# One engine order for the whole kernel: a list scheduler in the kernel in place of the built-in order (hybrid encoder layer, one core)

## The chip, the core and the metric

The kernel runs on one core of a Trainium2 chip. Five engines work side by side, each through its own queue in order: TensorE (PE in the profile; PEld is its weight loads), VectorE (DVE), ScalarE (ACT), GpSimd (POOL) and SyncE (SP, which here only issues DMAs). The metric is the device time of one execution in microseconds, lower is better.

## What is computed

One layer of a streaming encoder, for a prompt of 512 rows and a sample of 64 rows (together T = 576 columns) with shared weights, in fp32:

```python
D_MODEL = 1024; SEQ = 512; DEC_SEQ = 64; CHUNK = 64; N_MEM = 256; D_FF = 4096
xn = _rmsnorm(x, ln_mix);  proj = xn @ w_in
conv_in, z, a, b, qd, kd, vd = jnp.split(proj, SPLIT_AT, axis=-1)
c = jax.nn.silu(_causal_conv(conv_in, conv_w, conv_buf))            # 12 blocks of 128 channels
g = -jnp.exp(a_log) * jax.nn.softplus(a + dt_bias);  beta = jax.nn.sigmoid(b)
oa, S_new = _gdn_chunked(qa, ka, va, g, beta, S0)                    # gated delta rule, 4 heads, chunk by chunk
ob = _diff_attention(qd, k_all, v_all, q_pos, k_pos, lam)            # softmax minus lam * softmax, 4 heads
h = x + concat[rmsnorm(oa) * silu(z), rmsnorm(ob) * (1 - lam0)] @ w_out
h = h + _mem_attn(_rmsnorm(h, ln_mem_q), mem_k, mem_v, w_mem_q, w_mem_o)   # mem_k, mem_v from rmsnorm(mem_prompt)
h = h + jnp.square(jax.nn.relu(_rmsnorm(h, ln_ffn) @ w_ff1)) @ w_ff2
y = _rmsnorm(h, ln_final)
```

## The kernel before

Activations are held transposed (channels on partitions, 576 columns). Each fp32 operand of a large product is split into a high part and a rest, both in the fast fp32 form (`wh` and `wl` for weights, made from `raw` by a ScalarE cast on L159 and a VectorE subtraction on L160; `u_6`, `u_7` for the activations). `project` (L167) makes one block of 128 output channels in a PSUM bank with tag `pr`, in two halves of the columns: the first 256 with high and rest side by side (512 wide for `wh`, 256 for `wl`), and the other 320 one after the other. All matmuls are issued by `mm` (L107), all transposes by `tr` (L113), so the trace shows these two lines for nearly everything on TensorE, and the tile names tell the work: `pr` is a projection, `g0`, `g1` are the banks of the delta-rule preparation and later of the attention scores, `gs` the bank of the delta-rule scan and of the attention output, `ba` the transposes.

The stages in the profiled execution: to about 36 us the head block (norm of x, first projections), to 97 the convolution inputs, to 131 the gates and z, to 247 the delta rule (`gdn_prep` L653, `gdn_scan` L814) with projections beside it, to 357 the differential attention with the remaining input projections and the memory keys and values beside it, to 525 the output projection and the memory attention, to 945 the output of the memory attention and the feed-forward part, then the tail.

What sets the order of the work: the kernel issues instructions in program order, stage by stage, and a built-in scheduler reorders them on every engine by dependences, free buffers and priorities. The kernel steers it at a few places. `in_order` (L52, used once around the head block at L363) chains the instructions of a block on each engine as they are written; `tc.issue_after` (L430, L469, L477, L601, L609, L705, L848, L934, L956, L1458, L1660) keeps a block behind a given instruction; `tc.keep_in_program_order` (L109, L115, L133) pins some matmuls, transposes and two loads; `tc.high_priority` (L158 and others) favours casts. Buffers: three banks for `pr`, two for `ba`, one each for `g0`, `g1`, `gs`; three `raw`, two `wh` and two `wl`.

Lines that the prediction speaks of: L155 loads a weight block into `raw`; L261 to L267 load the small constants; L490 loads the gate columns of `w_in` (`wab`), L514 and L515 `dt_bias` and `a_log` into `dtb`, and L517 is the Exp of `a_log`; L133 loads a gain row for all partitions (`gB`, 512 KB); L286 casts the transposed activations of the head block into `u_6` and `u_7`; L645 belongs to the gates and z.

Of the kernel before, what the change touches and what calls it, by code (L numbers as in the profile page):

```python
# [15 lines left out]
P = 128  # L16
# [19 lines left out]

@with_exitstack
def hybrid_layer_kernel(
# [11 lines left out]

    @contextmanager
    def in_order():  # L52

        block = nc.cur_bb.bb.instructions
        first, last, ends = len(block), {}, {}
        yield ends
        for i in block[first:]:
            if i.engine in last:
                tc.add_manual_dep(
                    i, last[i.engine],  # L60
                    mybir.DependencyInfo(mybir.DependencyClass.NoSync, mybir.DependencyReason.DATA),
                    reason="in_order",
                )
# [3 lines left out]
    cp = ctx.enter_context(tc.tile_pool(name="cp", bufs=1))
    up = ctx.enter_context(tc.tile_pool(name="up", bufs=1))
    tp = ctx.enter_context(tc.tile_pool(name="tp", bufs=2))
    wp = ctx.enter_context(tc.tile_pool(name="wp", bufs=2))  # L70
# [35 lines left out]
    def mm(out, lhsT, rhs, start=True, stop=True, pin=False, skip_group_check=False):  # L106
        i = nc.tensor.matmul(out, lhsT, rhs, start=start, stop=stop, skip_group_check=skip_group_check)  # L107
        if pin:
            tc.keep_in_program_order(i)  # L109

    def tr(out, in_, pin=False):
        n = in_.shape[0]
        i = nc.tensor.transpose(out, in_, ident[:n, :n])  # L113
        if pin:
            tc.keep_in_program_order(i)  # L115
# [92 lines left out]
    def row_broadcast(rst, out, pin=False):  # L208

        b, b2 = bank(), bank()  # L210
        for t in range(5):
            o = b2[:, :P] if t == 4 else b[:, t * P : (t + 1) * P]
            mm(o, bc(rst[:, t : t + 1], [P, P]), ident, pin=pin and t % 4 == 0)
        A.copy(out[:, :SEQ], b)
        V.tensor_copy(out[:, SEQ:], b2[:, DEC:P])
        return out
# [146 lines left out]
    with in_order() as opened:  # L363
# [78 lines left out]
    for typ in (1, 0, 2):  # L442
        flat = (e5[:, 1], e2[:, 1], e2[:, 0])[typ].rearrange("p k t -> p (k t)")

        cT[typ] = [ap.rearrange("p (h t) -> p h t", h=H) for ap in (flat[:, : H * SEQ], flat[:, H * SEQ :])]
        for h in range(H):
            m = typ * 4 + h
            if m in FIRST:
                if m != FIRST[0]:
                    second(m)  # L450
            else:
                project(weights(w2, m * P), xs, conv_input(m))
            cb = cbs[m]
# [6 lines left out]
            last_v = nc.cur_bb.bb.instructions[-1]  # L460
# [16 lines left out]
    with tc.issue_after(behind_keys[1]):  # L477
# [117 lines left out]
    tc.keep_in_program_order(nc.sync.dma_start(mt, mem_prompt[0].rearrange("(b p) d -> p b d", p=P)))  # L595
# [5 lines left out]
    with tc.issue_after(behind_keys[1]):  # L601
# [7 lines left out]
    with tc.issue_after(last_v):  # L609
# [43 lines left out]
    def gdn_prep(c, nb, L):  # L653
# [34 lines left out]
        summed[c] = nc.cur_bb.bb.instructions[-1]  # L688
# [16 lines left out]
        with tc.issue_after(summed[0]):  # L705
            for i in range(nb):
                V.scalar_tensor_tensor(gam[:, i, :], bg[:, i, :], G_[:, i : i + 1], most, ALU.subtract, ALU.min)
# [106 lines left out]
    def gdn_scan(c, L, q, S):  # L814
# [32 lines left out]
        def finish():  # L847
            with tc.issue_after(summed[min(c + 2, 4)]):  # L848
                next(norm, None)
# [84 lines left out]
    with tc.issue_after(behind_keys[0]):  # L934
# [21 lines left out]
    with tc.issue_after(behind_keys[0]), tc.issue_after(behind_keys[1]):  # L956
# [389 lines left out]
    fp = ctx.enter_context(tc.tile_pool(name="fp", bufs=1, reuse_waits="tile"))  # L1346
# [124 lines left out]
    def ff1_pair(p, sx):  # L1471
# [58 lines left out]
        put_last[p] = nc.cur_bb.bb.instructions[-1]  # L1530
# [77 lines left out]
    def final_roots(ts, pin=False, more=None):  # L1608
# [3 lines left out]
        for i, t in enumerate(ts):  # L1612
            q0, n = QT[t]
            mm(b[:, t : t + 1], accs[0][:, q0 : q0 + n], ones[:, 0:1], pin=pin and i == 0)
# [38 lines left out]
    for g in range(1, NG):  # L1653
        nxt = odd() if g % 2 else pair(5, F32R)
        for m in range(KT):
# [3 lines left out]
            if g == 2:  # L1659
                with tc.issue_after(nc.cur_bb.bb.instructions[-1]):  # L1660
# [61 lines left out]
```

## Time and profile before

| | us |
|---|---|
| median of 3 runs | 970.83 (970.36 to 972.32) |
| the profiled execution | 972.5 |
| its span, first to last instruction | 968.8 |
| mean granted TensorE clock | 0.997 |

The times are those of whole executions; the profile is one execution with a span a little shorter than its time. Busy times of the engines overlap, so they don't add up to the span. A matmul's busy time is modelled from its start to the end of its pipeline, so two matmuls in a row overlap. What the rows show is given with the prediction. A row of the timeline is start, length, engine, line, operation, output<-inputs, shape and count; in brackets stand the idle time ahead of it and what ended it.

### The profile page before, as it was taken

Reading aid. Unit: us, or ns where it says so; the run is one execution under the profiler, and the core shown is the slowest. Engines: PE = TensorE matmul, PEld = TensorE weight load, DVE = VectorE, ACT = ScalarE, POOL = GpSimd, SP = SyncE. Lnnn points to the kernel's source line nnn. Section 1 sums busy time; section 2 is a strip of 40 time slices with the busy share of each in tenths; the row PEclk is TensorE's granted clock in tenths of the full one; section 3 lists DMA queues with packets and bytes.
Section 4 is the critical chain, followed back from the end, with each engine's and each line's share of the span. In section 5 each row is a group of like instructions: output and inputs, shape, how many; then the busy total and the mean of one; then the engine's idle time right before and its main releaser. Section 6 shows DMA issues by size and latency. Waiting matters only on the chain.

```text
span 968.8 us, 17030 instructions
## 1 busy us (share of the span) xinstructions
PE 954.5 (99%) x6399; PEld 888.5 (92%) x6399; DVE 689.6 (71%) x1538; ACT 541.3 (56%) x1248; POOL 66.9 (7%) x158
## 2 busy tenths in 40 slices
PE   9999999999999999999999999999999999999996
PEld 7999998998889878999999999999999999999996
DVE  6655777776867776666557977668867779978574
ACT  7664775533656765444445658666645554555444
POOL 4341020211010000000000000000000000000000
PEclk9999999999999999999999999999999999999998
DMA  7442342120643657332112423322322222323202
GB/s 210 123 134 77 87 134 66 38 72 22 177 133 105 224 175 220 87 112 64 44 44 65 123 66 116 90 88 87 88 88 87 88 88 87 88 88 87 66 23 97
DMA packets 124915, 96.01 MB, mean 99 GB/s; under 512 B 6204, under 2 KB 112846, under 8 KB 124322
## 3 DMA queue, kind: packets, MB, share of 16 engines
q1 hardware_dynamic: 124466, 94.28, 33.6%
q8 instruction: 50, 0.82, 0.4%
q10 hardware_dynamic: 368, 0.66, 0.2%
q14 instruction: 31, 0.25, 0.1%
HBM read 79.93 MB, written 9.75 MB: 93 GB/s over the span
## 4 chain that ended last, share of the span: by engine, by line
PE 61%; issue 2%; ACT 0%; POOLq 0%; POOL 0%; DVE 0%; ACTq 0%
PE pr L107 38%; PE ba L107 11%; PE g L107 7%; PE gs L107 4%; PE ba L113 1%; ACT u L1601 0%; POOLq L1718 0%; POOL tiny L206 0%; DVE u L1219 0%; ACTq L1606 0%; DVE tiny L1615 0%; POOLq L206 0%
## 5 line engine op out<-in xcount | busy, mean ns | idle before, releaser
L107 PE MATMUL pr<-u,wh 128*128 128x320 f32 (+2 forms) x1240 | 325.7, 341 | 0.3
L107 PEld LDWEIGHTS pr<-u,wh 128*128 128x128 f32 x1240 | 211.8, 188 | 15.4 <-ACT u L286 0.4
L107 PE MATMUL pr<-u,wl 128*128 128x256 f32 (+1 forms) x816 | 225.8, 300 | 0.0
L107 PEld LDWEIGHTS pr<-u,wl 128*128 128x128 f32 x816 | 150.3, 189 | 2.4 <-DVE wl L387 0.2
L160 DVE TENSOR_TENSOR wl<-raw,wh 128x1024 fp32r<-128x1024 f32 x65 | 79.5, 1224 | 56.4 <-ACT wh L159 56.2
L159 ACT CAST wh<-raw 128x1024 fp32r<-128x1024 f32 x65 | 68.3, 1051 | 61.2 <-PE pr L107 44.6
L107 PE MATMUL pr<-u,w2h 128*128 128x320 f32 (+1 forms) x384 | 96.7, 339 | 0.0
L107 PE MATMUL pr<-f,w2h 128*128 128x320 f32 (+1 forms) x288 | 72.4, 339 | 0.0
L1459 ACT CAST w2h<-r 128x512 fp32r<-128x512 f32 x56 | 34.8, 621 | 65.4 <-PE pr L107 64.1
L107 PEld LDWEIGHTS pr<-u,w2h 128*128 128x128 f32 x384 | 65.1, 188 | 4.3
L107 PE MATMUL pr<-u,w2l 128*128 128x256 f32 (+1 forms) x256 | 65.2, 295 | 0.0
L206 POOL TENSOR_TENSOR tiny<-tiny,nhalf 128x1 f32<-128x1 f32 (+4 forms) x10 | 8.9, 888 | 645.2 <-DVE tiny L1615 508.0
L107 PE MATMUL ba<-u,wl 128*128 128x288 f32 x360 | 52.7, 295 | 0.0
L107 PEld LDWEIGHTS pr<-f,w2h 128*128 128x128 f32 x288 | 48.8, 188 | 3.4 <-issue 0.2
L1549 DVE TENSOR_TENSOR u<-u,pr 128x256 f32<-128x256 f32 x96 | 43.3, 451 | 8.6 <-PE pr L107 7.9
L107 PEld LDWEIGHTS ba<-u,wl 128*128 128x128 f32 x360 | 49.4, 188 | 0.0
L107 PE MATMUL pr<-f,w2l 128*128 128x256 f32 (+1 forms) x192 | 48.8, 295 | 0.0
L107 PEld LDWEIGHTS pr<-u,w2l 128*128 128x128 f32 x256 | 47.0, 189 | 1.5
L1460 DVE TENSOR_TENSOR w2l<-r,w2h 128x512 fp32r<-128x512 f32 x56 | 38.6, 689 | 9.9 <-ACT w2h L1459 9.7
L107 PE MATMUL pr<-wh,u 128*128 128x512 f32 x128 | 41.6, 400 | 0.1
L107 PEld LDWEIGHTS pr<-f,w2l 128*128 128x128 f32 x192 | 35.2, 189 | 1.1
L1506 ACT ACTIVATE c<-c 128x288 f32<-128x288 f32 x48 | 20.3, 445 | 27.2 <-DVE c L1505 26.1
(552 smaller groups left out, 2027.6 us busy)
## 6 DMA issues: line engine op xcount, KB each, us to landing
raw<-in_w_ff_dram SPq DMA_DIRECT2D x36, 512.0 KB
raw<-in_w_in_dram SPq DMA_DIRECT2D x28, 512.0 KB
r<-in_w_ff_dram SPq DMA_DIRECT2D x56, 256.0 KB
raw<-in_w_mem_k_dram SPq DMA_DIRECT2D x8, 512.0 KB
raw<-in_w_mem_v_dram SPq DMA_DIRECT2D x8, 512.0 KB
raw<-in_w_out_dram SPq DMA_DIRECT2D x8, 512.0 KB
raw<-in_w_mem_q_dram SPq DMA_DIRECT2D x8, 512.0 KB
raw<-in_w_mem_o_dram SPq DMA_DIRECT2D x8, 512.0 KB
```

The source lines that it names most:

```text
L107: i = nc.tensor.matmul(out, lhsT, rhs, start=start, stop=stop, skip_group_check=skip_group_check)
L113: i = nc.tensor.transpose(out, in_, ident[:n, :n])
L159: A.copy(wh, raw)
L160: V.tensor_tensor(wl, raw, wh.bitcast(F32), ALU.subtract)
L206: G.tensor_tensor(out, in_, bc(nhalf[: in_.shape[0], 0:1], list(in_.shape)), ALU.pow)
L1459: A.copy(wh, src)
L1460: V.tensor_tensor(wl, src, wh.bitcast(F32), ALU.subtract)
L1506: A.activation(c, c, AF.Relu)
L1549: V.tensor_tensor(am, am, b, ALU.add)
```

## The change

The hints to the built-in scheduler become data, and a scheduler inside the kernel fixes the order of every engine. `in_order` and the new `after` only note chains of instruction names; the pins are gone; pools are wrapped so that each tile's pool, tag and number of buffers are known. At the end of the program `arrange` builds a `Step` for every traced instruction, with its reads and writes, its dependences and an estimated duration, runs a simulated clock over all engines, always taking the instruction that can start first (among those that can start by then on that engine, the one with the best priority, then the earliest in the program), and pins the resulting order of each engine with dependences that carry no semaphore. The number of matmuls, transposes, DMAs, VectorE and GpSimd instructions stays what it was; ScalarE's table loads go from 15 to 13.

The core of the diff:

```diff
+class Step:
...
+    def cost(self):
...
+        if self.engine == "PE":
...
+            self.fetch = 105.0 if self.turn else max(105.0 * w.size / 128, 55.0)
...
+            by_size = {512: 235.0 if len(x.dims) > 2 else 229.0, 384: 175.0, 320: 146.5, 288: 132.5, 256: 119.0}
...
+        elif self.engine == "ACT":
+            self.time = (155 if bank else 190) + 0.84 * n + 100 * (len(self.ins) > 1) + 60 * (len(self.outs) > 1)
+        elif self.engine == "DVE":
...
+                self.time = 145 + 1.06 * n + 62 * (column and self.op == "TensorScalarPtr")
+        else:
+            power = self.op == "TensorTensor" and any(a.tile.startswith("nhalf") for a in self.ins)
+            by_op = dict(TensorTensor=(185, 2.2), TensorScalarPtr=(185, 2.2), TensorScalarAffineSelect=(150, 1.8))
+            base, rate = (500, 140) if power and n <= 16 else by_op.get(self.op, (100, 0.85))
+            self.time = base + rate * n
...
+class Arrangement:
...
+        for _ in range(len(todo)):
+            start, engine = min((self.start(s), e) for e in engines for s in self.queue[e])
+            s = min((s for s in self.queue[engine] if self.start(s) <= start), key=lambda s: (s.priority, s.n))
+            self.queue[engine].remove(s)
+            self.open_tiles(s)
+            end = self.execute(s)
...
+    def start(self, s):
+        at = s.ready
+        for t in s.tiles:
+            at = max(at, self.opened[t] if t in self.opened else min(self.slots[self.place[t][0]]["free"]) + 33)
...
+        if s.engine == "PE":
+            began, step = self.last
+            return max(began + step, max(began, at) + s.fetch)
+        return max(self.clock[s.engine], at)
+
+    def execute(self, s):
...
+        if s.is_dma:
+            self.clock[s.engine] = at + 400
+            begin = max(at + 1300, self.wire)
+            self.wire = begin + s.bytes / 240.0
+            return max(self.wire + 500, at + 1900)
+        if s.engine == "ACT":
+            table = dict(Silu="Silu", Exp="Exp").get(str(getattr(s.inst, "func", "")).split(".")[-1])
+            if table not in (None, self.table):
+                self.table = table
+                at += 1300
+        self.clock[s.engine] = at + s.time - OVERLAP[s.engine]
+        return at + s.time + 10
...
+def arrange(tc, instructions, homes, chains, closing, opening):
+    for instructions_of_engine in Arrangement(instructions, homes, closing, opening, chains).run().values():
+        for earlier, later in zip(instructions_of_engine, instructions_of_engine[1:]):
+            tc.add_manual_dep(
+                later, earlier.name,
+                mybir.DependencyInfo(mybir.DependencyClass.NoSync, mybir.DependencyReason.DATA),
+                reason="arrange",
+            )
...
+    chains, opened = [], {}
+
     @contextmanager
     def in_order():
...
+        for i in block[first:]:
+            engines.setdefault(i.engine, []).append(i.name)
+        chains.extend(engines.values())
+        opened.update((e, names[-1]) for e, names in engines.items())
...
+    def after(*earlier):
+
         block = nc.cur_bb.bb.instructions
...
+        first = len(block)
+        yield
+        chains.extend((e, i.name) for i in block[first:] for e in earlier)
...
-    def mm(out, lhsT, rhs, start=True, stop=True, pin=False, skip_group_check=False):
-        i = nc.tensor.matmul(out, lhsT, rhs, start=start, stop=stop, skip_group_check=skip_group_check)
-        if pin:
-            tc.keep_in_program_order(i)
...
+    def mm(out, lhsT, rhs, start=True, stop=True, skip_group_check=False):
+        nc.tensor.matmul(out, lhsT, rhs, start=start, stop=stop, skip_group_check=skip_group_check)
...
-        tc.keep_in_program_order(nc.sync.dma_start(gB, g.partition_broadcast(P)))
+        nc.sync.dma_start(gB, g.partition_broadcast(P))
...
-    with tc.issue_after(opened[mybir.EngineType.Pool]):
+    with after(opened[mybir.EngineType.Pool]):
...
+
+    arrange(tc, nc.cur_bb.bb.instructions, homes, chains, closing="sp", opening="fp")
```

Below, lines of the changed kernel differ from those of before: L107 is L407 there, L113 is L411, L159 is L455, L286 is L582, L517 is L813.

**TensorE in the delta rule** (around 231 to 238 us in the profile before). `g1_360` to `g1_363` are steps of the preparation of one chunk, `gs_417` and `gs_419` of the scan, `g0_3..` of the preparation of the next chunk, `pr_5..` projections. Before:

```order
L107 MATMUL pr_539_3120<-u_7_92,wh_534_3092 128x320
L113 MATMUL g1_361_2269<-ident_79,Dt1_343_2185 128x128 x4
L113 MATMUL g0_397_2395<-ident_79,X_393_2389 128x128 x2
L107 MATMUL g1_362_2276<-Dt1_343_2185,At1_335_2160 64x64 x4
L107 MATMUL g1_363_2282<-X_341_2183,Y1_342_2184 64x64 x4
L113 MATMUL g0_399_2402<-ident_79,Y0_394_2390 128x128
L107 MATMUL g0_399_2402<-Dt0_395_2391,B0_398_2400 128x128
L107 MATMUL gs_417_2476<-on_416_2474,X_341_2183 128x128 x3
L107 MATMUL g0_400_2407<-Y0_394_2390,X_393_2389 128x128
L107 MATMUL gs_417_2476<-on_416_2474,X_341_2183 128x128
L107 MATMUL gs_419_2483<-S_267_1889,u_4_78 128x128
```

Now:

```order
L407 MATMUL g0_386_2369<-u_1_75 128x128
L411 MATMUL g1_361_2269<-ident_79,Dt1_343_2185 128x128 x4
L407 MATMUL g0_386_2369<-u_1_75 128x128
L407 MATMUL gs_415_2469<-S_267_1889,u_1_75 128x128 x3
L407 MATMUL g1_362_2276<-Dt1_343_2185,At1_335_2160 64x64 x4
L407 MATMUL g0_388_2375<-u_4_78,u_1_75 128x128 x2
L407 MATMUL gs_415_2469<-S_267_1889,u_1_75 128x128
L407 MATMUL g1_363_2282<-X_341_2183,Y1_342_2184 64x64 x4
L407 MATMUL pr_530_3047<-u_7_92,wl_526_3017 128x320
```

and, behind it, from `gs_417` to `gs_419`:

```order
L407 MATMUL gs_417_2476<-on_416_2474,X_341_2183 128x128 x2
L407 MATMUL pr_536_3096<-u_6_91,wl_535_3093 128x256
L407 MATMUL pr_536_3096<-u_6_91,wh_534_3092 128x512
L407 MATMUL pr_536_3096<-u_6_91,wl_535_3093 128x256
L407 MATMUL pr_536_3096<-u_6_91,wh_534_3092 128x512
L407 MATMUL pr_536_3096<-u_6_91,wl_535_3093 128x256
```

Projections 530 and 536 now stand among these steps, with the scan step `gs_415` and the preparation of the next chunk; before, the projections had ended at the first of these rows. Between the last row shown and `gs_419` stand seven more rows, among them five of `pr_536`.

**TensorE in the attention** (around 283 us before). `ba_551` transposes the scores of one head, a ScalarE copy makes `aT_552` from it, and `gs_553` multiplies that by the values. Before:

```order
L107 MATMUL ba_551_3184<-both_2546,p1_550_3178 128x128 x3
L107 MATMUL pr_622_3523<-u_7_92,wh_617_3495 128x320
L107 MATMUL pr_622_3523<-u_7_92,wl_618_3496 128x320
L107 MATMUL pr_622_3523<-u_7_92,wh_617_3495 128x320 x2
L107 MATMUL pr_622_3523<-u_7_92,wl_618_3496 128x320 x2
L107 MATMUL pr_622_3523<-u_7_92,wh_617_3495 128x320 x2
L107 MATMUL pr_684_3751<-u_6_91,wh_682_3747 128x512
L107 MATMUL pr_684_3751<-u_6_91,wl_683_3748 128x256
L107 MATMUL pr_684_3751<-u_6_91,wh_682_3747 128x512
L107 MATMUL gs_553_3190<-u_2_76,aT_552_3185 128x128 x2
```

Now, from the row behind `ba_551` on:

```order
L407 MATMUL pr_684_3751<-u_7_92,wh_682_3747 128x512
L407 MATMUL pr_685_3772<-u_6_91,wh_682_3747 128x320 x2
L407 MATMUL pr_685_3772<-u_6_91,wl_683_3748 128x320
L407 MATMUL pr_685_3772<-u_6_91,wh_682_3747 128x320 x2
L407 MATMUL pr_685_3772<-u_6_91,wl_683_3748 128x320
L407 MATMUL pr_685_3772<-u_6_91,wh_682_3747 128x320 x2
L407 MATMUL pr_685_3772<-u_6_91,wl_683_3748 128x320
L407 MATMUL pr_685_3772<-u_6_91,wh_682_3747 128x320 x2
L407 MATMUL pr_685_3772<-u_6_91,wl_683_3748 128x320
L407 MATMUL pr_685_3772<-u_7_92,wh_682_3747 128x320 x2
L407 MATMUL pr_685_3772<-u_7_92,wl_683_3748 128x320
L407 MATMUL gs_553_3190<-u_2_76,aT_552_3185 128x128 x2
```

Eight matmuls of 320 columns and three of `pr_684` stood in between; now fifteen of 320 and one of 512.

**ScalarE in the head block** (20 to 25 us before). `u_6` and `u_7` with `gs_49` and `g1_50` are the activations of the last 64 columns; `tiny_136` is the Exp of `a_log`. Before:

```order
L286 CAST u_6_91<-pr_46_282 128x4x128
L286 CAST u_7_92<-ba_47_287 128x4x128
L286 CAST u_6_91<-gs_49_307 128x4x64
L286 CAST u_7_92<-g1_50_312 128x4x64
L316 COPY p0_51_321<-pr_40_235 128x256
L316 COPY an_52_346<-pr_48_298 128x256
```

Now:

```order
L582 CAST u_6_91<-pr_46_282 128x4x128
L582 CAST u_7_92<-ba_47_287 128x4x128
L813 ACTIVATE tiny_136_1155<-dtb_1152 128x4
L582 CAST u_6_91<-gs_49_307 128x4x64
L582 CAST u_7_92<-g1_50_312 128x4x64
L612 COPY p0_51_321<-pr_40_235 128x256
L612 COPY an_52_346<-pr_48_298 128x256
```

The Exp, row 32 of ScalarE before, stands ahead of the two casts. On SP the loads of L490, L514 and L515 (dt_bias, a_log) and the 512 KB of `gB` now stand ahead of the first three `raw` loads of L155 (raw_60, raw_75, raw_82), behind which they stood.

More of the change, by code (lines that the diff above doesn't have):

```diff
@@ L34, with __init__, meets, covers @@
 ROWS = [slice(0, P)] * 4 + [slice(DEC, P)]
+ENGINES = {"PE": "PE", "DVE": "DVE", "Activation": "ACT", "Pool": "POOL", "SP": "SP"}
+OVERLAP = dict(ACT=99.0, DVE=83.0, POOL=60.0)
+BANK_TAGS = ("pr", "ba", "g0", "g1", "gs")
+class Access:
+    def __init__(self, ap, write):
+        t = ap.tensor
+        self.write, self.tile = write, t.name
+        self.on_chip = "DRam" not in type(t).__name__
+        self.dims = [(int(s), int(n)) for s, n in ap.ap]
+        self.size = 1
+        for _, n in self.dims[1:]:
+            self.size *= n
+        self.bank = self.on_chip and t.name.split("_")[0] in BANK_TAGS
+        if not self.on_chip:
+            self.rows, self.columns = (0, 1 << 20), 1
+            return
+        width = 1
+        for n in t.shape[1:]:
+            width *= int(n)
+        p0, first = divmod(int(ap.offset), width)
+        self.rows = (p0, p0 + self.dims[0][1])
+        dims, run = self.dims[1:], 1
+        while dims and dims[-1][0] == run:
+            run *= dims.pop()[1]
+        starts = [first]
+        for s, n in dims:
+            starts = [x + s * k for x in starts for k in range(n)]
+        self.columns = 0
+        for x in starts:
+            self.columns |= (1 << run) - 1 << x
+    def meets(self, other):
+        return (
+            (self.write or other.write) and self.rows[0] < other.rows[1] and other.rows[0] < self.rows[1]
+            and self.columns & other.columns != 0
+        )
+    def covers(self, other):
+        return (
+            self.write and self.rows[0] <= other.rows[0] and other.rows[1] <= self.rows[1]
+            and other.columns & ~self.columns == 0
+        )
@@ L67, in hybrid_layer_kernel @@
[L67 to L70, printed above, removed]
+        block, engines = nc.cur_bb.bb.instructions, {}
+        first = len(block)
[4 more added lines that the diff above has]
+        opened.update((e, names[-1]) for e, names in engines.items())
@@ L212, in row_broadcast @@
             o = b2[:, :P] if t == 4 else b[:, t * P : (t + 1) * P]
-            mm(o, bc(rst[:, t : t + 1], [P, P]), ident, pin=pin and t % 4 == 0)
+            mm(o, bc(rst[:, t : t + 1], [P, P]), ident)
         A.copy(out[:, :SEQ], b)
@@ L474, in hybrid_layer_kernel @@
                 nc.sync.dma_start(hd[i], hst[i])
-    with tc.issue_after(behind_keys[1]):
+    with after(behind_keys[1]):
         ones2, triu2 = const([P, P], "ones2"), const([P, P], "triu2")
@@ L600, in hybrid_layer_kernel @@
     near_ = [t for u in (small("X", [P, 4, P]), small("X", [P, 4, P])) for t in (u[:, 0, :], u[:, 1, :], u[:, 2, :])]
-    with tc.issue_after(behind_keys[1]):
+    with after(behind_keys[1]):
         for lb, e in enumerate(near_):
@@ L608, in hybrid_layer_kernel @@
     lev = const([P, P], "lev")
-    with tc.issue_after(last_v):
+    with after(last_v):
         V.tensor_scalar(lev, ident, -1.0, 64.0, ALU.mult, ALU.add)
@@ L704, in gdn_prep @@
         gam = st("gam")
-        with tc.issue_after(summed[0]):
+        with after(summed[0]):
             for i in range(nb):
@@ L847, in finish @@
         def finish():
-            with tc.issue_after(summed[min(c + 2, 4)]):
+            with after(summed[min(c + 2, 4)]):
                 next(norm, None)
@@ L931, in hybrid_layer_kernel @@
     sample = gdn_scan_sample(prepared[4], S)
-    with tc.issue_after(behind_keys[0]):
+    with after(behind_keys[0]):
         lv4 = small("zr", [P, 4, 64])
@@ L955, in hybrid_layer_kernel @@
     both = const([P, P], "both")
-    with tc.issue_after(behind_keys[0]), tc.issue_after(behind_keys[1]):
+    with after(*behind_keys):
         G.memset(qz[64:, :64], 0.0)
@@ L1457, in split @@
         wh, wl = (ft(tag + x, shape, bufs, F32R) for x in "hl")
-        with tc.high_priority() if urgent else tc.issue_after(put_last[1]):
+        with tc.high_priority() if urgent else after(put_last[1]):
             A.copy(wh, src)
@@ L1590, in turn_out @@
         for i in range(4):
-            tr(b[:, i * P : (i + 1) * P], hT[half][:, i, q0 : q0 + n], pin=pin and i == 0)
+            tr(b[:, i * P : (i + 1) * P], hT[half][:, i, q0 : q0 + n])
         return b
@@ L1613, in final_roots @@
             q0, n = QT[t]
[L1614 removed]
+            mm(b[:, t : t + 1], accs[0][:, q0 : q0 + n], ones[:, 0:1])
         V.tensor_scalar(r[:, c], b[:, c], 1.0 / D, EPS, ALU.mult, ALU.add)
@@ L1659, in hybrid_layer_kernel @@
             if g == 2:
-                with tc.issue_after(nc.cur_bb.bb.instructions[-1]):
+                with after(last_traced()):
                     square_block(m)
```

232 lines of the change are left out of this document (200 added, 32 removed).

## Prediction

> **What bounds the kernel now.** I read the engine totals of the page first, then the chain that ended last, then a table of stretches (busy us of each engine, with the count of instructions behind it), and last the timeline of the stretches that stand out.
>
> ```profile
> span 968.8 us, 17030 instructions
> PE 954.5 (99%) x6399; PEld 888.5 (92%) x6399; DVE 689.6 (71%) x1538; ACT 541.3 (56%) x1248; POOL 66.9 (7%) x158
> PE 61%; issue 2%; ACT 0%; POOLq 0%; POOL 0%; DVE 0%; ACTq 0%
> ```
>
> TensorE is the bound: it is busy 954.5 of 968.8 us and it alone carries the chain. The change keeps every matmul, so time can only come out of stretches in which TensorE stands or runs below its pace. The idle time by this count is 968.8 - 954.5 = 14.3 us, but a matmul's busy time includes its pipeline, so a stretch can be full by this count and still have lost time. I therefore need the pace.
>
> ```profile
> 23.90 1.34 PE L107 MATMUL pr<-u,wh 128*128 128x320 f32 x8
> 25.07 1.34 PE L107 MATMUL pr<-u,wl 128*128 128x320 f32 x8
> ...
> 286.32 0.39 PE L107 MATMUL pr<-u,wh 128*128 128x512 f32 x1
> 286.55 0.28 PE L107 MATMUL pr<-u,wl 128*128 128x256 f32 x1
> ...
> 240.72 0.61 PE L107 MATMUL ba<-vn,kd 128*128 128x128 f32 x4
> 241.17 0.29 PE L113 MATMUL g<-ident,Y 128*128 128x128 f32 x1
> ```
>
> The columns are start and length in us. Undisturbed, eight matmuls of 320 columns take 25.07 - 23.90 = 1.17 us, 0.146 each; one of 512 takes 0.23 (286.32 to 286.55) and one of 256 half of that; four of 128 columns take 0.45, 0.112 each.
>
> ```profile
> 125.00:150.00 25.00, 24.71 (x184) 23.34 (x183) 22.60 (x54) 18.55 (x39) 6.26 (x10) 1.00 0.32 81
> 150.00:175.00 25.00, 24.88 (x196) 22.56 (x195) 16.81 (x40) 13.03 (x32) 1.69 (x6) 1.00 0.20 51
> 175.00:200.00 25.00, 25.00 (x192) 23.59 (x190) 20.85 (x47) 10.96 (x25) 6.05 (x10) 1.00 0.30 75
> 200.00:225.00 25.00, 24.97 (x201) 23.17 (x200) 19.34 (x49) 9.12 (x24) 4.63 (x10) 1.00 0.13 33
> 225.00:250.00 25.00, 22.35 (x168) 19.36 (x167) 18.04 (x51) 12.42 (x37) 3.14 (x9) 1.00 0.29 82
> 232.00:246.00 14.00, 11.43 (x90) 9.60 (x91) 8.54 (x26) 7.58 (x24) 1.62 (x4) 1.00 0.25 65
> 250.00:275.00 25.00, 24.93 (x162) 22.05 (x161) 19.62 (x69) 15.79 (x54) 0.16 (x1) 1.00 0.63 162
> 275.00:300.00 25.00, 24.36 (x157) 21.83 (x156) 16.37 (x53) 14.49 (x49) 2.62 (x6) 1.00 0.42 118
> 300.00:325.00 25.00, 24.82 (x165) 22.01 (x164) 18.68 (x62) 17.19 (x57) 1.53 (x3) 1.00 0.63 196
> 325.00:350.00 25.00, 24.94 (x142) 20.15 (x141) 17.41 (x51) 17.78 (x56) 1.53 (x3) 1.00 0.55 171
> 350.00:375.00 25.00, 24.21 (x119) 19.52 (x117) 17.10 (x21) 15.70 (x26) 1.36 (x2) 1.00 0.56 176
> 525.00:945.00 420.00, 420.00 (x2873) 405.56 (x2872) 322.51 (x651) 236.26 (x516) 0.00 (x0) 1.00 0.29 85
> ```
>
> After the stretch and its length the columns are TensorE, its weight loads, VectorE, ScalarE and GpSimd, then the granted clock (1.00 throughout) and DMA. I added up the matmuls of each stretch at the paces above. In 232 to 246, 74 matmuls of 128 columns and 16 of 64 (half as long, about 0.06) make 74 x 0.112 + 16 x 0.06 = 9.3 us, so 4.7 of 14.0 us are lost, of which only 2.6 shows as idle. The same sum gives as lost: 125 to 150 0.8; 150 to 175 2.6; 175 to 200 1.0; 200 to 225 1.8; 225 to 250 6.4; 250 to 275 2.5; 275 to 300 3.5; 300 to 325 1.9; 325 to 350 1.6; 350 to 375 1.4. That is 6.2 us in 125 to 225, 6.4 in 225 to 250 and 10.9 in 250 to 375. In 525 to 945 (the feed-forward part with the projection ahead of it) the sum comes out within 1.7 us of 420: that stretch is at its floor. So 23 us, all of it before 375, are what an order can win; it can't win them all, because the recurrences have a latency.
>
> [...]
>
> **The change part by part.** *The hole at 232 to 246* is the largest term.
>
> ```profile
> 231.57 0.39 PE L107 MATMUL pr<-u,wh 128*128 128x320 f32 x1
> ...
> 233.59 0.68 PE L107 MATMUL g<-Dt,At 128*64 128x64 f32 x8 [0.60 <-ACT X L776]
> 234.82 0.65 PE L107 MATMUL g<-X,Y 128*64 128x64 f32 x8 [0.55 <-ACT Y L782]
> ...
> 238.17 0.49 PE L107 MATMUL gs<-S,u 128*128 128x128 f32 x2 [0.78 <-DVE vn L833]
> ...
> 245.60 0.48 PE L107 MATMUL pr<-u,wh 128*128 128x512 f32 x1
> ```
>
> The last projection matmul stands at 231.57 and the next at 245.60; between them TensorE has only the delta-rule chains, and waits for each of their ACT and DVE steps. The new order keeps projections 530, 536 and 539 back and lays them between the same chain steps. From the rows shown with the change: between g1_361 and g1_362 stood two transposes (0.22 us), now four matmuls (0.45); between g1_362 and g1_363 nothing, now three (0.34); between gs_417 and gs_419 nothing, now some 2 us of pr_536. The neighbour 200 to 225, which has chains and filler mixed, loses 1.8; I let this stretch come down to that: 6.4 - 1.8, about **-4.5 us**. Bounds: 0 (the filler taken away leaves as much of a hole where it stood) and -6.4.
>
> *250 to 375.* Here two places can be read.
>
> ```profile
> 283.72 0.40 PE L107 MATMUL pr<-u,wh 128*128 128x512 f32 x1
> 284.76 0.68 PE L107 MATMUL gs<-u,aT 128*128 128x128 f32 x4 [0.64 <-ACT wh L159]
> ...
> 356.99 0.50 PE L107 MATMUL pr<-wl,u 128*128 128x512 f32 x1 [0.69 <-DVE wl L160]
> 357.59 0.73 PE L107 MATMUL pr<-wh,u 128*128 128x512 f32 x2
> ```
>
> At 284.76 gs_553 starts 1.04 us after the matmul before it, 0.8 more than that one's 0.23; the ScalarE copy it needs stood behind a weight cast. Between ba_551 and gs_553 stood 8 x 0.146 + 2 x 0.23 + 0.11 = 1.74 us of projection, now 15 x 0.146 + 0.23 = 2.42: -0.7. At 356.99 and 357.59 TensorE waits 0.84 and 0.37 us above pace, first for a weight residual that DVE computes; now that residual stands ahead of its DVE neighbours (-1.0). The other 10.9 - 2.0 = 8.9 us are many short stalls; I take a quarter, which is a choice, 2.2. Together **-3.9**, bounds 0 and -8.
>
> *125 to 225.* The stalls are many and short. Their chain steps move 3 to 11 us ahead among the projections, and the memory norm moves out of this part altogether, which frees ScalarE and VectorE here. Of 6.2 I take a quarter, a choice as above: **-1.5**, bounds +1 and -4. Two table loads disappear as well:
>
> ```profile
> L645 ACT ACT_TABLE_LOAD x5 | 6.4, 1283 | 0.1
> ```
>
> At 1283 ns each that is 2.6 us of ScalarE, which has slack there (18.55 of 25 busy at most), so 0 for the sum; if that cover fails it is up to -2.6, inside the bounds.
>
> *The head* is where the new order gives something back.
>
> ```profile
> 19.16 3.59 SPq L155 DMA_DIRECT2D raw<-in_w_in_dram  x3
> 22.81 0.96 SPq L490 DMA_DIRECT2D B<-in_w_in_dram  x1
> 23.82 1.67 SPq L514 DMA_DIRECT2D dtb<-in_dt_bias_dram  x1
> 25.53 0.46 SPq L515 DMA_DIRECT2D dtb<-in_a_log_dram  x1
> ...
> 22.02 0.38 ACT L286 CAST u<-g 128x256 fp32r<-128x256 f32 x1
> 29.89 0.19 ACT L517 ACTIVATE tiny<-dtb 128x4 f32<-128x4 f32 x1
> ...
> 0.79 0.65 SPq L249 DMA_DIRECT2D B<-in_ln_mix_dram  x2
> 2.38 0.50 PEld L107 LDWEIGHTS g<-B,ones 1*128 1x128 f32 x2 [0.22 <-DMA B<-in_ln_mix_dram]
> ```
>
> ScalarE's Exp of a_log stood at 29.89 and now stands ahead of the two casts that ended at 22.40, which the projection at 23.90 reads. Queued behind it on ScalarE are those casts and two copies of accumulators; who waits is TensorE. On SP the load of a_log now comes ahead of raw_60, raw_75 and raw_82, but behind the loads of lines 490 and 514. It is issued at the earliest at 19.16 + 0.96 and, if these loads keep their lengths, by 19.16 + 0.96 + 1.67 + 0.46 = 22.3. A small load took some 1.4 us from issue to use at 2.38. It lands then at 21.5 to 23.7; Exp and casts (0.19 + some 0.65) are done by 22.4 to 24.6, against 23.90: 0 to **+0.7**; 1.67 was measured behind 1.5 MB of weights, so I take **+0.4**. [...]
>
> The gain broadcast (512 KB) also goes ahead of raw_60; it delays weights used from 27.66 on by under 2 us, which I count as hidden by the projections at 23.90 to 31; uncovered it would cost up to 2.
>
> *New waits.* An order fixed from estimated durations leaves some consumers closer to their producers than before. No row shows this; nearest are the stalls above, 0.4 to 1 us each. I take a handful, **+2**, bounds 0 and +6.
>
> Sum: -4.5 - 3.9 - 1.5 + 0.4 + 2 = **-7.5 us**. The profiled execution took 972.5 us (span 968.8 and 3.7 around it) and would take 965.0. It stands 1.7 above the median of 970.83, so the forecast for the median is **963.3 us**.
>
> **The rivals.** *The stalls only move.* Filler is a fixed sum of matmuls, and what is laid into 232 to 246 is missing from 172 to 210, or the hole reopens at 250. For it: the lost 23 us come from chains whose length doesn't change. Against it: 200 to 225 loses just 1.8 with both kinds mixed, and chain steps were brought 3 to 11 us forward into that filler. Only the two read waits of 250 to 375 would remain: -1.7 + 0.4 = -1.3, 969.5 us.
>
> *The whole gap closes.* The order also finds cover for the short stalls: three quarters of 23 us is 17, less 2 of new waits and 0.4 in the head, some -14: 957 us. For it: filler is plentiful until 400. Against: softmax and recurrence steps wait in turn for VectorE.
>
> *Slower, because VectorE sets the pace.* VectorE is busy 79.6 of 100 us in 125 to 225, with 22.60 of 25 at the start. Chains brought forward load it earlier, and a pinned queue can't pass a late instruction. If its instructions run longer than the formulas, everything pinned behind slips; 5% of 79.6 is 4 us, and from about 10% (8 us) on the gain is gone; at 14% the time is +3.5, 974 us.
>
> ```profile
> L160 DVE TENSOR_TENSOR wl<-raw,wh 128x1024 fp32r<-128x1024 f32 x65 | 79.5, 1224 | 56.4 <-ACT wh L159 56.2
> ```
>
> Against it: the formula gives 145 + 1.06 x 1024 = 1230 ns where this row, the costliest of VectorE, has 1224.
>
> *The change does nothing:* the built-in order would have to be left standing; the listed orders differ on all engines, so I give it next to nothing.
>
> **How the numbers follow.** Chances: forecast (4 to 12 us won) 0.57; whole gap 0.10; stalls move 0.20; slower 0.13. The measurement can tell about 0.2%, 1.9 us, from no change. Half of "stalls move" lies beyond that on the fast side only if it wins 2 us or more; I give that 0.08 of its 0.20 and 0.12 to no change. Faster 0.75, same 0.12, slower 0.13. The range reaches from the likelier whole-gap time, 957, to just above no change, 971.5; it leaves out about 0.13 above and 0.05 below.
>
> **What would show it.** Right: the gap between projection matmuls in the delta-rule part is gone and no stretch of 14 us holds under 11.5 us of weight loads; the waits at gs_553 and at pr_792's residual are gone; span 961 to 962. Wrong: the casts before 23.9 end after 24 (head worse than +0.7); TensorE idle above 14 us; new waits for DVE in 125 to 225; the feed-forward part longer than before, for which I count nothing.

## The result, and the profile after

| | before | changed |
|---|---|---|
| median, us | 971.11 (4 runs, 970.36 to 972.32) | 958.46 (4 runs, 957.96 to 960.24) |
| ratio | | 0.9872, 95% interval 0.9855 to 0.9889 |
| the profiled execution, us | 972.5 | 958.01 |
| its span, us | 968.8 | 956.1 |

The changed kernel is 1.3% faster, 12.7 us by the spans. The page of the changed kernel, span, engine totals and the chain that ended last:

```profile
span 956.1 us, 17017 instructions
PE 945.9 (99%) x6399; PEld 889.0 (93%) x6399; DVE 690.8 (72%) x1538; ACT 536.4 (56%) x1246; POOL 68.2 (7%) x158
PE 92%; DMA 2%; issue 2%; DVE 2%; ACT 1%; POOL 0%; SPq 0%; POOLq 0%; ACTq 0%; DVEq 0%
```

The work is the same (weight loads 889.0 us against 888.5) and the span is shorter. TensorE has 92% of the span in the chain that ended last. The 61% of before can't be set beside it: that chain could be followed back only to 357.59 us, the present one to 1.48. The same stretches as before the change (length; TensorE, its weight loads, VectorE, ScalarE, GpSimd; clock; DMA):

```profile
125.00:150.00 25.00, 25.00 (x192) 24.07 (x191) 21.63 (x56) 17.45 (x41) 4.96 (x8) 1.00 0.27 73
150.00:175.00 25.00, 25.00 (x206) 23.28 (x205) 17.08 (x42) 10.70 (x23) 4.47 (x10) 1.00 0.21 53
175.00:200.00 25.00, 25.00 (x194) 23.92 (x193) 22.67 (x53) 11.10 (x26) 4.79 (x8) 1.00 0.21 54
200.00:225.00 25.00, 25.00 (x210) 23.58 (x208) 17.25 (x47) 11.00 (x29) 3.98 (x10) 1.00 0.18 43
225.00:250.00 25.00, 25.00 (x183) 23.58 (x182) 18.05 (x49) 14.25 (x41) 1.62 (x4) 1.00 0.68 175
250.00:275.00 25.00, 23.99 (x165) 22.03 (x164) 17.74 (x57) 15.09 (x51) 1.03 (x2) 1.00 0.48 123
275.00:300.00 25.00, 25.00 (x169) 23.08 (x167) 19.62 (x64) 15.86 (x55) 2.56 (x6) 1.00 0.34 93
300.00:325.00 25.00, 25.00 (x165) 22.21 (x163) 17.34 (x59) 17.83 (x59) 2.90 (x5) 1.00 0.84 260
325.00:350.00 25.00, 25.00 (x140) 21.07 (x139) 21.84 (x50) 19.23 (x53) 1.36 (x2) 1.00 0.48 159
350.00:375.00 25.00, 25.00 (x125) 21.27 (x124) 16.50 (x20) 13.47 (x20) 0.00 (x0) 1.00 0.75 225
525.00:945.00 420.00, 420.00 (x2886) 406.41 (x2885) 319.26 (x645) 234.51 (x515) 0.70 (x1) 1.00 0.29 86
```

Nine of the ten short stretches are full; 225 to 250 holds 23.58 us of weight loads where it held 19.36. The longest time from one projection matmul's start to the next between 215 and 250 us is 4.1 us, where it was 14.0:

```profile
228.56 0.48 PE L407 MATMUL pr<-u,wh 128*128 128x512 f32 x1
...
232.64 0.36 PE L407 MATMUL pr<-u,wl 128*128 128x256 f32 x1
```

What is left of waits on TensorE (waiting line, what for, us in total, times, longest):

```profile
PE gs L407 <- POOL ones L440: 1.2, 1, 1.2
PE g L407 <- DMA Dt<-At: 1.0, 1, 1.0
PE ba L407 <- DVE gg L845: 0.2, 1, 0.2
```

Added up against the paces of the prediction, the time lost by TensorE (us, by stretches of the span) is in the profiled execution of each kernel (the medians beside it are over all executions; in sp_free and pe_only the profiled one took 1.5 us less):

| | 0-25 | 25-125 | 125-225 | 225-250 | 250-375 | 375-525 | 525- | sum | median, us |
|---|---|---|---|---|---|---|---|---|---|
| before | 7.2 | 2.4 | 6.2 | 6.3 | 10.8 | 3.1 | 1.6 | 37.7 | 971.1 |
| changed | 7.9 | 2.7 | 4.6 | 1.5 | 5.2 | 2.0 | 1.4 | 25.2 | 958.5 |
| old_gdn_pe | 7.2 | 2.9 | 4.5 | 7.6 | 7.6 | 2.0 | 1.5 | 33.2 | 966.2 |
| old_attn_pe | 7.4 | 2.8 | 4.7 | 2.2 | 19.7 | 1.8 | 1.5 | 40.1 | 973.3 |
| pe_only | 7.3 | 2.8 | 8.6 | 2.6 | 12.0 | 2.6 | 4.3 | 40.2 | 974.5 |
| all_but_pe | 7.7 | 3.1 | 6.7 | 3.1 | 8.8 | 1.6 | 1.4 | 32.4 | 965.1 |
| sp_free | 7.2 | 10.3 | 3.9 | 1.9 | 7.2 | 1.9 | 1.6 | 34.0 | 968.3 |
| flat_times | 7.0 | 2.0 | 16.0 | 9.5 | 35.3 | 16.7 | 7.2 | 93.7 | 1028.5 |
| dve_short | 7.9 | 2.9 | 9.1 | 2.2 | 8.3 | 3.6 | 2.7 | 36.7 | 969.5 |
| dma_late | 7.6 | 2.2 | 4.5 | 1.3 | 7.8 | 2.3 | 1.4 | 27.2 | 960.0 |
| tail_first | 7.3 | 2.5 | 4.1 | 6.2 | 5.3 | 2.0 | 1.5 | 28.9 | 962.1 |
| margin | 7.7 | 2.2 | 2.9 | 9.8 | 5.8 | 1.1 | 1.4 | 30.9 | 963.7 |
| margin40_late | 7.4 | 2.5 | 3.5 | 3.8 | 8.2 | 0.9 | 1.4 | 27.7 | 960.6 |

Span less this sum is 931 us in each of the first three (968.8 - 37.7, 956.1 - 25.2, 964.2 - 33.2): the matmuls are the same, so a difference in span is time that TensorE loses in one of these stretches. The table says where; the cause has to come from elsewhere.

### The profile page after: what moved, and what is told of

The parts are those of the page before. It is cut to its first block, busy times and chain, and to the rows that moved or that the text cites. A ratio compares the mean times of both kernels' runs of the same rounds, so it can differ in the third digit from the quotient of the medians.

```text
span 956.1 us, 17017 instructions
## 1 busy us (share of the span) xinstructions
PE 945.9 (99%) x6399; PEld 889.0 (93%) x6399; DVE 690.8 (72%) x1538; ACT 536.4 (56%) x1246; POOL 68.2 (7%) x158
## 4 chain that ended last, share of the span: by engine, by line
PE 92%; DMA 2%; issue 2%; DVE 2%; ACT 1%; POOL 0%; SPq 0%; POOLq 0%; ACTq 0%; DVEq 0%
PE pr L407 57%; PE ba L407 12%; PE g L407 12%; PE gs L407 7%; PE ba L411 2%; PE g L411 2%; DMA KQ<-vb 1%; DMA Dt<-At 1%; DMA u<-in_x_prompt_dram 0%; DMA out_dram<-p 0%; PE pr L411 0%; DVE wl L456 0%; DVE p L755 0%; ACT u L1897 0%; PE gs L411 0%
## 5 line engine op out<-in xcount | busy, mean ns | idle before, releaser
L407 PE MATMUL pr<-u,wh 128*128 128x320 f32 (+2 forms) x1240 | 326.3, 341 | 0.0
L407 PE MATMUL pr<-u,wl 128*128 128x256 f32 (+1 forms) x816 | 225.5, 301 | 0.0
L407 PEld LDWEIGHTS pr<-u,wh 128*128 128x128 f32 x1240 | 211.2, 188 | 14.4 <-ACT u L582 0.4
L407 PEld LDWEIGHTS pr<-u,wl 128*128 128x128 f32 x816 | 149.9, 189 | 2.6 <-DVE wl L683 0.2
L455 ACT CAST wh<-raw 128x1024 fp32r<-128x1024 f32 x65 | 68.2, 1049 | 74.4 <-PE pr L407 63.9
L407 PE MATMUL pr<-u,w2h 128*128 128x320 f32 (+1 forms) x384 | 96.7, 339 | 0.0
L407 PE MATMUL pr<-f,w2h 128*128 128x320 f32 (+1 forms) x288 | 72.3, 339 | 0.0
L407 PEld LDWEIGHTS pr<-u,w2h 128*128 128x128 f32 x384 | 65.1, 188 | 4.3
L407 PE MATMUL pr<-u,w2l 128*128 128x256 f32 (+1 forms) x256 | 65.2, 295 | 0.0
L407 PE MATMUL ba<-u,wl 128*128 128x288 f32 x360 | 52.7, 295 | 0.0
L407 PEld LDWEIGHTS pr<-f,w2h 128*128 128x128 f32 x288 | 48.8, 188 | 3.3
L1845 DVE TENSOR_TENSOR u<-u,pr 128x256 f32<-128x256 f32 x96 | 42.8, 446 | 11.2 <-PE pr L407 10.8
L407 PEld LDWEIGHTS ba<-u,wl 128*128 128x128 f32 x360 | 49.4, 188 | 0.0
L407 PE MATMUL pr<-f,w2l 128*128 128x256 f32 (+1 forms) x192 | 48.8, 295 | 0.0
L407 PEld LDWEIGHTS pr<-u,w2l 128*128 128x128 f32 x256 | 47.0, 189 | 1.5
L407 PE MATMUL pr<-wh,u 128*128 128x512 f32 x128 | 42.0, 399 | 0.0
L1515 DVE TENSOR_TENSOR u<-u,pr 128x256 f32<-128x256 f32 (+1 forms) x48 | 21.6, 451 | 20.4 <-PE pr L407 20.4
L407 PEld LDWEIGHTS pr<-f,w2l 128*128 128x128 f32 x192 | 35.2, 189 | 1.1
```

Of the source, the lines that this page charges most:

```text
L455: A.copy(wh, raw)
L1515: V.tensor_tensor(hm, hm, b, ALU.add)
L1845: V.tensor_tensor(am, am, b, ALU.add)
```

## The experiments

All edit the changed kernel.

**old_gdn_pe and old_attn_pe: TensorE's old order in one part.** A list of the matmuls of that part, in the order of the kernel before, is added as one more chain; the scheduler then arranges all other work anew around it, so rows of ScalarE, VectorE and SyncE move too.

```diff
+    chains.append(as_before(instructions))
     for instructions_of_engine in Arrangement(instructions, homes, closing, opening, chains).run().values():
```

> The changed kernel, with one more chain: the matmuls that TensorE issued from 195 to 246 us in the kernel before keep that order; all else is arranged by the list scheduler. Theory A (the gain of the delta-rule part is filler laid among the chain steps on TensorE): the hole comes back, about 5 us longer than the changed kernel, 963 to 964 us, with a stretch of some 14 us without projection matmuls that loses 4 to 5 us against its pace. Rival B (what helps is that the producers stand earlier in the queues of VectorE and ScalarE, TensorE's order only follows): under 1.5 us lost, 958.5 to 960 us.

> The same with the matmuls of 246 to 375 us of the kernel before in their old order on TensorE. Theory A: most of the 5.6 us that this part gained between the two traces goes, 962.5 to 964.5 us. Rival B: the waits there were made by the order on ScalarE and VectorE (a copy behind a weight cast, a residual behind two other subtractions), so at most 2 us come back, 958.5 to 960.5 us.

The first took 966.2 us, 7.8 more than the changed kernel: theory A's direction, and 2 us more than it gave. The hole is back, 225 to 250 of this run:

```profile
225.00:250.00 25.00, 21.89 (x158) 18.12 (x157) 18.06 (x50) 11.79 (x36) 2.55 (x7) 1.00 0.30 77
```

Weight loads fall from 23.58 to 18.12 us; no projection starts for 14.7 us; the stretch loses 7.6 where it lost 1.5, and another 2.4 go in the attention behind it. The second took 973.3, more than theory A and far more than B, and more than the kernel before. Its two longest waits that the changed kernel hasn't, or has shorter:

```profile
PE g L450 <- DMA vb<-vb: 3.1, 1, 3.1
PE g L450 <- DMA Dt<-At: 1.7, 1, 1.7
```

An old order of TensorE among new orders of the others loses 19.7 us in 250 to 375, where the old order among the old ones lost 10.8. That is neither theory. The 8.9 us on top are nearly covered by these two waits for transfers (4.8), which the kernel before hasn't, and by the granted clock, which was 0.50 for 3.4 us behind each of them:

```profile
252.99:256.41 3.42, 3.42 (x15) 3.05 (x14) 1.96 (x7) 1.52 (x6) 0.00 (x0) 0.50 0.08 14
...
328.09:331.50 3.41, 3.22 (x14) 2.50 (x14) 0.76 (x5) 1.90 (x7) 0.15 (x1) 0.50 0.34 118
```

By the clock column 6.8 us at 0.50 do the work of 3.4, an estimate (in sp_free, below, eight matmuls at 0.50 took 2.30 us instead of 1.17); that makes 8.2 with the waits. By this sum, what went wrong is mostly that TensorE in its old order comes to two transfers before they are there: the orders of the engines have to fit each other. How much of the 5.6 us won in this stretch is due to TensorE's own order, the run doesn't tell.

**pe_only, all_but_pe and sp_free: which queues have to be pinned.** Some engines get the scheduler's order, the others the built-in one with the chains of the hints.

```diff
+    order = Arrangement(instructions, homes, closing, opening, chains).run()
+    by_name = {i.name: i for i in instructions}
+    pinned = [order["PE"]] + [[by_name[n] for n in chain] for chain in chains]
+    for instructions_of_engine in pinned:
```

(all_but_pe: `for e in ("ACT", "DVE", "POOL", "SP")`; sp_free: `for e in ("PE", "ACT", "DVE", "POOL")`.)

> The list scheduler's order is pinned on TensorE alone; the other four engines get the built-in order, with the chains of the hints. Theory A: nearly all of the gain stays, 958 to 960.5 us. Rival B: most of it goes, 965 to 971 us, since TensorE then waits at fixed places for producers that come in another order.

> The list scheduler's order is pinned on ScalarE, VectorE, GpSimd and SyncE; TensorE gets the built-in order, with the chains of the hints. Theory C, formed after TensorE's order alone came out slower than before (974.5 us): no single queue holds the gain, it is that all queues agree on one order; then this loses most of it too, 965 to 975 us. Rival B (the queues of the producers hold it): 958 to 961 us.

> All queues pinned but SyncE's, whose DMA issues get the built-in order with the chains of the hints. Theory: loads are issued well ahead of their use, so their order decides little, 958 to 961 us. Rival C in its strict form (every queue must agree): 964 us or more, with TensorE waiting for transfers.

pe_only took 974.5 us, slower than before: theory A falls, B's direction holds and even its upper end was too low. Its longest waits:

```profile
PE ba L410 <- DVE tiny L1947: 2.6, 1, 2.6
PE ba L414 <- DVE p L1404: 2.1, 2, 1.4
PE g L414 <- ACT B L981: 2.0, 2, 1.4
PE g L410 <- ACT p L1399: 1.8, 3, 0.9
```

TensorE stands at a fixed place while VectorE and ScalarE come to its operand in another order; one such wait, 2.6 us, lies in the feed-forward part, where the changed kernel has none. all_but_pe took 965.1: half of the gain, as theory C has it, at its near end. With either half alone the gain shrinks or turns. A and B in their pure forms don't stand; theory C does, though the producers' queues alone keep half.

sp_free took 968.3 us, against the first theory. The loss is almost all in one place, the head (7.6 of 8.8 us by the spans; another wait, 2.6 us for p<-in_cache_diff_k_dram, lies at 250 us). SyncE, ScalarE and TensorE there:

```profile
25.76 0.46 SPq L814 DMA_DIRECT2D dtb<-in_a_log_dram  x1
...
28.44 0.20 ACT L816 ACTIVATE tiny<-dtb 128x4 f32<-128x4 f32 x1 [7.44 <-DMA dtb<-in_a_log_dram]
28.55 0.35 ACT L585 CAST u<-gs 128x256 fp32r<-128x256 f32 x1
...
28.96 2.50 PE L410 MATMUL pr<-u,wh 128*128 128x320 f32 x8 [4.96 <-ACT u L585]
```

This is the wait that the prediction's head term was about. ScalarE's Exp stands ahead of the casts, the built-in order loads a_log behind three weight blocks (25.76), and TensorE stands for 5.0 us. The clock column of the same run tells why 7.6 us more are lost in 25 to 125 and not 5:

```profile
24.00:29.00 5.00, 0.04 (x2) 0.04 (x1) 0.06 (x1) 0.56 (x3) 0.00 (x0) 0.83 0.79 199
29.00:30.00 1.00, 1.00 (x4) 1.00 (x5) 1.00 (x3) 0.73 (x3) 0.00 (x0) 0.50 0.18 57
...
33.00:34.00 1.00, 1.00 (x6) 1.00 (x5) 0.00 (x0) 0.00 (x0) 0.00 (x0) 0.50 0.00 0
```

After the idle time the granted clock was 0.50 to 34 us; eight matmuls took 31.26 - 28.96 = 2.30 us instead of 1.17. The clock was at 0.50 from about 27.3 us (an estimate from the mean of 0.83 in 24 to 29, if it was 1.00 until then) to 34, and TensorE was at work again in the last 5 us of that. In margin, below, the clock was 0.50 for 3.4 us too, with no wait longer than 1.0 us ahead of it.

**flat_times and dve_short: how good the durations have to be.**

```diff
             self.cost()
+            if self.engine in ("ACT", "DVE", "POOL") and not self.is_dma:
+                self.time = 600.0
```

(dve_short: `if self.engine == "DVE": self.time *= 0.9`.)

> The list scheduler plans with 600 ns for every instruction of ScalarE, VectorE and GpSimd in place of the fitted durations; matmuls and DMAs as they were; all queues pinned. Theory D (the fit matters: an order that is right for wrong durations makes waits): 966 to 975 us. Rival (any order on which all queues agree and that lays filler among the chains does): 958 to 962 us.

> The list scheduler plans with VectorE times 10% shorter than the fitted ones, so that real instructions run 11% longer than planned. The prediction's rival priced this: the gain is used up at about 10%; from the sum as it turned out (12 us won) that would be 966 to 971 us. If queues and free time take up a tenth: 958 to 962 us.

flat_times took 1028.5 us, 57 more than before, beyond theory D's own range: the kernel with one consistent but badly informed order is the slowest of all. TensorE from 175 to 375 us of that run:

```profile
175.00:375.00 200.00, 169.04 (x1093) 147.01 (x1091) 118.20 (x331) 86.19 (x249) 18.13 (x42) 0.93 0.31 87
```

It is busy 169 of 200 us there, at a clock of 0.93; before it was 195.6. A mean of 0.93 over 200 us would be 28 us at a clock of 0.50, if the rest was at 1.00, and some 14 us of the loss; that is an estimate from the mean alone. dve_short took 969.5 us: an error of a tenth on one engine gives back 11 of the 12.7 us, 4.5 of them in 125 to 225 and 3.1 in 250 to 375. No wait of it is over half a microsecond except the first one of the kernel, which all runs have; it is lost in many small ones. Part of the 11 may come from the mere reshuffling: dma_late, tail_first, margin and margin40_late below keep the fitted durations of the engines and lose 1.5 to 5.2 us with their new orders.

**dma_late, tail_first, margin, late_mem_v and margin40_late: can the rest be had?** Edits of the plan:

```diff
-            return max(self.wire + 500, at + 1900)
+            return max(self.wire + 500, at + 1900) + 3000
...
-            s = min((s for s in self.queue[engine] if self.start(s) <= start), key=lambda s: (s.priority, s.n))
+            s = min((s for s in self.queue[engine] if self.start(s) <= start), key=lambda s: (s.priority, -self.tail.get(s.n, 0.0), s.n))
...
-                    t.ready = max(t.ready, end + (0 if s.boundary or t.boundary else 60 if t.engine == "POOL" else 33))
+                    t.ready = max(t.ready, end + (0 if s.boundary or t.boundary else 160 if t.engine == "POOL" else 133))
...
-        nc.sync.dma_start(cv_, src_[:, j % 2 * 512 : (j % 2 + 1) * 512])
+        with after(stack_end[0], stack_end[1]):
+            nc.sync.dma_start(cv_, src_[:, j % 2 * 512 : (j % 2 + 1) * 512])
```

The first is dma_late, the second tail_first (`tail` is the longest chain of planned time behind a step), the third margin, the fourth late_mem_v (`stack_end[h]` is the last of the copies that stack the keys of head h); margin40_late joins the fourth with 40 ns in place of the 100 of the third.

> The scheduler's model lets every DMA land 3 us later than in the changed kernel; nothing else. Theory A (the one new wait of the changed kernel, 1.0 us idle for the transfer Dt<-At at 253 us, is a mis-modelled latency): the wait goes and the time falls by about 1 us, 957 to 958 us. Rival: the order is reshuffled everywhere and other waits take its place, 958.5 to 961 us.

> The list scheduler takes, among instructions that can start, the one with the longest chain of work behind it, where it took the earliest in the program (the priority still comes first). If the 5 to 6 us that TensorE still loses in 225 to 300 us is a matter of choice among ready instructions: 953 to 957 us. If it is chain latency and transfers: within 1.5 us of 958.5, or worse up to 964 us, because buffers open in another order.

> The list scheduler plans with 100 ns more for every hand-over from one engine to another. If the short waits that are left (no single one above 0.3 us but for the transfer) come from orders that are too tight: 955 to 957.5 us. If the plan's errors are not in the hand-over: 958 to 962 us.

> The changed kernel with one more chain: the four loads of the cached memory values (256 KB each, two of which the list scheduler issues at 239 and 242 us, though nothing reads them before 400 us) come behind the copies that stack the keys of the first two heads. Theory: the transfer Dt<-At, on which TensorE waits 1.0 us at 253 us, came late because the DMA engines were full from 240 to 251; 512 KB less at some 270 KB per us bring it 1.9 us earlier, the wait goes, 957 to 957.8 us. Rival: the wait is the latency of the chain of copies, or the order shifts elsewhere: 958 to 960 us.

> The changed kernel with the late loads of the cached memory values and 40 ns more (not 100) for every hand-over in the plan. With 100 ns the projections 530 to 539 had moved ahead of the delta-rule steps again, as in the kernel before; with 40 ns the last of them stands behind the first steps of the scan step gs_419, as in the changed kernel. Theory E (225 to 250 is decided by where this filler stands against these steps): the stretch loses 1.5 to 3.5 us against its pace, and with the small gains that the margin of 100 ns had elsewhere (1 to 2 us) the kernel takes 956 to 959 us. Rival (the margin itself makes the hole): 7 us or more lost there, 962 us or more.

dma_late took 960.0: the wait for Dt<-At went, but 250 to 375 loses 7.8 instead of 5.2; the rival was right. tail_first took 962.1, inside its second theory (chains and buffers, not choice), and margin 963.7, slower than either of its theories. Both lose it by one hole: 6.2 and 9.8 us lost in 225 to 250, where the order has the projections run out and none starts for 14.1 and 19.8 us. In margin the clock adds to it:

```profile
240.20:243.61 3.41, 1.81 (x12) 1.31 (x13) 3.29 (x13) 2.30 (x10) 1.38 (x3) 1.00 0.62 146
243.61:247.03 3.42, 3.42 (x14) 3.07 (x14) 2.96 (x7) 2.18 (x6) 0.00 (x0) 0.50 0.82 231
```

TensorE was busy 1.81 of 3.41 us, and in the next 3.42 us the granted clock was 0.50, which is worth 1.7 of the 9.8 us, an estimate from that clock. Outside that stretch margin is 2.6 us better than the changed kernel. In margin40_late the longest such time is 3.9 us and the stretch loses 3.8, a little over theory E's range and far from its rival; 250 to 375 gave the rest back, and at 960.6 us the kernel missed the expected time. Over the seven orders before, changed, old_gdn_pe, margin, tail_first, margin40_late and late_mem_v the stretch loses 1.5 to 3.8 us where filler lasts and 6.2 to 9.8 where it runs out; that this placement decides it is shown best by old_gdn_pe, where it alone was imposed; in the others all queues moved.

In late_mem_v the wait for the transfer shrank, as expected, but not for the expected reason:

```profile
PE g L407 <- ACT p L1399: 3.2, 1, 3.2
PE gs L407 <- POOL ones L440: 1.2, 1, 1.2
PE ba L407 <- DVE gg L845: 0.3, 1, 0.3
PE g L407 <- DMA Dt<-At: 0.2, 1, 0.2
```

From 1.0 to 0.2 us. The transfer and its use, in the changed kernel and in late_mem_v:

```profile
246.84 1.11 SPq L1309 DMA_DIRECT2D Dt<-At  x2
253.47 0.42 PE L407 MATMUL g<-Dt,qs 128*128 128x128 f32 x2 [1.01 <-DMA Dt<-At]
...
245.83 1.10 SPq L1567 DMA_DIRECT2D B<-in_cache_mem_v_dram  x2
247.03 1.11 SPq L1311 DMA_DIRECT2D Dt<-At  x2
253.52 0.42 PE L407 MATMUL g<-Dt,qs 128*128 128x128 f32 x2 [0.24 <-DMA Dt<-At]
```

The chain moved the two loads from 239 and 242 us to 245.83, which is still ahead of the transfer, and that came no earlier: 6.6 us from issue to use in the changed kernel, 6.5 here. The wait is shorter because TensorE has more to do before it: its last projection matmul ahead of it starts at 252.99 instead of 252.06. So the run doesn't test whether the full DMA engines make the transfer late. Against it as the whole cause: in the changed kernel their mean share is 0.98 from 250 to 251 us, but 0.09 from 252 to 253, and the transfer is still not used before 253.47. The cause stays open.

The profiled execution was the one of five that took 964.1 us. Its extra wait of 3.2 us comes from ScalarE, which stood 4.5 us for an output store; behind it two matmuls of 512 columns started 0.43 us apart (311.46 and 311.89) where 0.23 is the pace, and the mean granted clock of this execution is 0.994 where the other four have 0.997 or 0.998. By these means the lower clock is worth another 3 to 4 us of its span of 962.1, an estimate. The other four took 957.4 to 958.5. At a median of 958.23 (ratio 0.9873, 0.9851 to 0.9896) it can't be told from the changed kernel. No version was measured that clearly beats it.

## Why the prediction was right, and what was mis-sized

The forecast was 963.3 us, 7.5 under the median; 12.7 was won, inside the range of 957 to 971.5, but just above the 4 to 12 us that had the chance of 0.57. Of the signs named for being right, the gap between projections is gone, the two waits are gone, and the stretch of 14 us poorest in weight loads (from 350 us) holds 11.5 us, just the limit; the span is below the 961 to 962. By its own terms:

- **225 to 250, -4.5.** Measured -4.8 (6.3 to 1.5). Right in place, mechanism and size: old_gdn_pe undoes it and loses 6.1 there. The lower bound of 0, that the hole only moves, didn't happen in the changed order, but in margin and tail_first the hole stayed.
- **250 to 375, -3.9.** Measured -5.6. The two waits that were read are gone. The quarter taken of the other 8.9 us was too little: (5.6 - 1.7) / 8.9 is 44%. This fraction was a choice, and is one of the two terms that failed in size.
- **125 to 225, -1.5.** Measured -1.6.
- **The head, +0.4.** 7.2 to 7.9 by the trace, but old_gdn_pe, with the same order there, loses 7.2; the difference starts with a weight load used at 8.58 instead of 8.26 us, ahead of the reordered part. One of the signs named for being wrong came up: the casts end after 24 us. They still cost TensorE nothing, by a small margin: it came to them 0.65 us later than before itself, at 24.55 instead of 23.90:

```profile
20.04 0.42 SPq L811 DMA_DIRECT2D dtb<-in_a_log_dram  x1
...
23.58 0.20 ACT L813 ACTIVATE tiny<-dtb 128x4 f32<-128x4 f32 x1 [1.87 <-DMA dtb<-in_a_log_dram]
23.95 0.38 ACT L582 CAST u<-g 128x256 fp32r<-128x256 f32 x1
...
24.55 1.34 PE L407 MATMUL pr<-u,wh 128*128 128x320 f32 x8
```

  ScalarE stood 1.87 us for a_log, the casts ended at 24.33, and TensorE came to them at 24.55. The landing took 3.1 us from the end of the issue, more than the 1.4 that I took (the row at 2.38, counted the same way, gives 0.9: issues from 0.79 to 1.44). But the loads ahead were issued faster than assumed (0.39 and 0.58 us, not 0.96 and 1.67). The under 2 us by which the gain broadcast was to delay weights is an estimate from the rate of before: 512 KB at the 279 GB/s of 24 to 26 us are 1.9 us. What I put at +0.7 for the worst case is 5.0 us of standing when SyncE's order doesn't fit (sp_free).
- **New waits, +2.** The second term that failed: there is one, 1.0 us for Dt<-At at 253 us, and it is already inside the -5.6.
- **Not counted:** 375 to 525 gave 1.1, 25 to 125 took 0.3.

So the step that failed is the size of two terms that no row carried, both chosen towards no gain, 2 us each. Of the rivals, "the whole gap closes" came nearest in time (957) though TensorE still loses 11.3 of 23.3 us in 125 to 375. The price in "VectorE sets the pace", gain gone from about 10% error, was tested by dve_short and nearly holds in the sum (11.0 of 12.7 us lost, 969.5 us), but not in place: only 4.5 of it lies in 125 to 225, where the rival put it all. Its condition didn't come about: the fitted times were good enough.

## What to carry to other kernels

A kernel whose bound engine idles between dependent chains gains by laying independent work among them, but in full only when every queue is ordered for it: TensorE's good order alone among the others' built-in ones was slower than the start (974.5 us against 971.1), and all queues but TensorE's kept half (965.1). A planned order is as good as its durations, so measure them first; a plan with a tenth off on one engine lost nearly all of the gain here. Look for the place where the independent work runs out before the chain does, and check it again after each change of the plan, because small edits move it.

## What the runs showed of the hardware

An idle time of 5.0 us on TensorE cost 7.6 in sp_free, since the granted clock was 0.50 for the 5 us after it (29 to 34 us); eight matmuls of 320 columns took 2.30 us there instead of 1.17. In margin the granted clock was 0.50 from 243.61 to 247.03 us, behind 3.41 us in which TensorE was busy 1.81 us with no wait longer than 1.0 us among them. A transfer of 128 KB (Dt<-At, changed kernel) took 6.6 us from issue to use (246.84 to 253.47), with a mean share of the DMA engines of 0.98 to 1.18 in each microsecond from 246 to 251 and of 0.09 from 252 to 253. A load of 2 KB (a_log, changed kernel) took 3.1 us from the end of its issue at 20.46 us to its use at 23.58.
